# TensorE's order in a planned two-block network: float32 matmuls gathered, a turn of type charged, sums of one bank in order

## The chip, the core and the metric

The kernel runs on one core of a Trainium2 chip. The metric is the device time of one execution in microseconds (us). The kernel before was timed three times: 2192.33, 2192.88 and 2197.85 us, the median is 2192.88 us.

## What is computed

One sequence of 256 tokens of width 1024 passes through two residual blocks of two layers each, all in float32. Each layer is a feed-forward network of 2816, a mixer, and a second feed-forward network.

```python
def first_block(x, ...):                       # twice (DEPTH = 2)
    h = rmsnorm(x, ffn1_pre_g[l])
    x = x + 0.5 * rmsnorm(swiglu(h, ffn1_w_gate[l], ffn1_w_up[l], ffn1_w_down[l]), ffn1_post_g[l])
    h = rmsnorm(x, mix_pre_g[l])
    m = hybrid_mixer(h, w_in[l], w_out[l], ...)   # gated delta net, differential attention, SSD, mLSTM
    x = x + rmsnorm(m, mix_post_g[l])
    ...                                           # ffn2 as ffn1
def second_block(x, c, w_ada, b_ada, ...):     # twice
    mod = cond @ w_ada[l] + b_ada[l]              # nine rows of shifts, scales and gates
    y = _swiglu(_modulate(x, sh1, sc1), ffn1_w_gate[l], ffn1_w_up[l], ffn1_w_down[l])
    x = _post_norm(x, y, g1, FFN_RES, ln_gain[l, 0], ln_bias[l, 0])
    y = _token_mixer(_modulate(x, sh2, sc2), w_in[l], w_out[l])  # retention, dilated and stick-breaking attention
    ...
```

## The kernel before

Weights come from memory in units of 128 x 1024 (tiles `raw`, `R`, `S`), fetched by SyncE's queue. ScalarE rounds each unit to float32r (`wH`), VectorE takes the difference (`wL`), and activations are split likewise (`hT`, `A`, `B`, `X`: a high and a low part each). Every large product is then three float32r matmuls (`mm3`, `ws3`: high by high, high by low, low by high), summed in one PSUM bank. These are 12408 of the program's 13728 matmuls. The other 1320 read float32: 444 transposes with the identity (`tr<-con,h` and the like, 128 x 128) and 876 small products of the mixers. Of these small products 628 use a part of the array (64 rows by 64 columns in the gated delta net, 32 or 64 rows in the attentions), the others all 128 x 128 of it. A float32 product that is not a transpose has two records in the trace.

PSUM banks have names by use: `pa`, `pb` for the feed-forward sums, `pj` for the mixers' projections, `pg` and `po` for the small products and the last projection of a mixer, `tr` for transposes. The mixers' code is a set of generators (`gdn`, `diff`, `ssd`, `mlstm`; `retention`, `dilated`, `stick`) woven between the projections, so that float32r matmuls stand between the links of their chains of small products.

No instruction is issued while this code runs. `Program` records every operation as an `Op` with its engine, the time that it occupies it (`occ`), the time until its result (`done`; both from `taken`) and what it must follow. `emit` then plans: `ranks` gives each operation the longest way from it to the end, with TensorE's operations tied in their present order; `place` puts all operations on timelines of the engines by rank; TensorE's order is then sorted by the planned starts, and this is done four times (`ROUNDS`). The best plan's starts order the instructions of all engines, and each engine runs its own in that order. So a table of costs and the rules of `emit` set the order of every engine, DMA issues too. All recorded operations carry one source line, that of `getattr(...)` in `Engine.__getattr__`.

Before the change, the line that orders TensorE anew at the end of a round is

```python
pe = sorted(pe, key=lambda o: (o.start, o.i))
```

and a float32r matmul of m columns is charged `max(0.12, m / 2400 + 0.0127)` us: 0.12 at 256 columns, 0.226 at 512.

Of the kernel before, what the change touches and what calls it, by code (L numbers as in the profile page):

```python
# [13 lines left out]
F32R = mybir.dt.float32r  # L14
# [3 lines left out]
PSUM = bass.MemoryType.PSUM  # L18
# [166 lines left out]
class Tile:  # L185


    def __init__(self, pool, name, shape, dt, tag, bufs):
        self.pool, self.name, self.shape, self.dt, self.tag, self.bufs = pool, name, shape, dt, tag, bufs
        self.space = PSUM if pool is not None and tag in Program.banks else None  # L190
        self.size = math.prod(shape[1:]) + -math.prod(shape[1:]) % 8
        self.host, self.at = None, 0
        self.ap, self.seen, self.gates, self.gate, self.ops = None, [], None, None, []

    def real(self):
        if self.ap is None:
# [64 lines left out]


class Op:
    __slots__ = ("i", "eng", "run", "occ", "done", "before", "after", "start", "end", "rank", "size", "ins", "outs")

    def __init__(self, i, eng, run, occ, done, size=0):
        self.i, self.eng, self.run, self.occ, self.done, self.size = i, eng, run, occ, done, size
        self.ins, self.outs = (), ()
        self.before, self.after, self.start, self.end, self.rank = {}, [], 0.0, 0.0, 0.0


class Program:
# [147 lines left out]
    def touch(self, op, v, write):  # L420
        t = v.tile
        held = t
        if t.pool is None:
            r = 0, 1, v.offset, v.offset + sum(s * (n - 1) for s, n in v.ap) + 1
        else:
            r = Clock.region(v)
        if t.host is not None:
            held = t.host
            r = (r[0], r[1], r[2] + t.at, r[3] + t.at)
        if write and held.gates is not None:  # L430
            g = held.gates
            if g.gate is None:
                g.gate = self.add(None, None)
                for u in g.ops:
                    self.after(g.gate, u)
            self.after(op, g.gate, 0.0)
        keep = []
        for q, o, w in held.seen:
            hit = q[0] < r[1] and r[0] < q[1] and q[2] < r[3] and r[2] < q[3]
            if hit and o is not op and (write or w):  # L440
                same = o.eng == op.eng == "pe"
                self.after(op, o, o.occ if same else None)
            if not (write and hit and r[0] <= q[0] and q[1] <= r[1] and r[2] <= q[2] and q[3] <= r[3]):
                keep.append((q, o, w))
        keep.append((r, op, write))
        held.seen = keep
# [13 lines left out]
    def ranks(self, pe):  # L460
        for op in self.ops:
            op.after = []
        for op in self.ops:
            for o, lag in op.before.items():
                o.after.append((op, lag))
        nxt = {a: b for a, b in zip(pe, pe[1:])}
        self.sorted = self.topo(nxt)
        for op in reversed(self.sorted):
            r = op.done
            for o, lag in op.after:  # L470
                r = max(r, lag + self.flight(op) + o.rank)
            if op in nxt:
                r = max(r, op.occ + nxt[op].rank)
            op.rank = r

    @staticmethod
# [23 lines left out]
    def place(self):  # L500

        free = {e: Timeline() for e in ("pe", "act", "dve", "pool", "sp", "actq", "wire")}
        for op in sorted(self.sorted, key=lambda o: -o.rank):
            t = 0.0
            for o, lag in op.before.items():
                t = max(t, o.start + (o.end - o.start - o.done) + lag)
            if op.eng is None:
                op.start, op.end = t, t
                continue
            op.start = free[op.eng].take(t, op.occ)  # L510
            op.end = op.start + op.done
            if op.size:
                b = op.size / DMA_RATE
                at = free["wire"].take(op.start + DMA_FIRST, b)
                op.end = at + b + DMA_LAST
        return max(op.end for op in self.ops)

    def emit(self):
        self.rooms()
# [2 lines left out]
        self.says = []  # L522
        best = None
        for _ in range(ROUNDS):
            self.ranks(pe)
            end = self.place()
            self.says.append(round(end, 1))
            if best is None or end < best[0]:
                best = (end, {op: op.start for op in self.ops})
            pe = sorted(pe, key=lambda o: (o.start, o.i))  # L530
        start = best[1]
        with self.tc.manual_schedule(), \
                self.tc.tile_pool(name="psum", bufs=1, space=PSUM, reuse_waits="tile") as self.psum.live, \
# [32 lines left out]
def taken(kind, name, outs, ins, a, k):  # L566

    n = max(math.prod(x.shape[1:]) for x in outs + ins)
    if kind == "pe":
# [1 line left out]
        if name == "transpose":  # L571
            return 0.11, 0.31
        if ins[1].dtype == F32R:
            occ = max(0.12, m / 2400 + 0.0127)
            return occ, occ + 0.2
        rows = ins[0].shape[0]
        occ = 2 * max(0.112, m / 1200 + 0.01)
# [35 lines left out]
}  # L613

LAG = 0.06
ROUNDS = 4
DMA_RATE = 0.3e6
DMA_FIRST, DMA_LAST = 0.3, 1.7
# [2 lines left out]
class Engine:  # L621
# [5 lines left out]
    def __getattr__(self, name):  # L627
        def call(*a, after=0.0, **k):
# [16 lines left out]
                op = self.prog.add(eng, run, 0.06, 0.06, size)  # L645
            else:
                op = self.prog.add(self.kind, run, *taken(self.kind, name, outs, ins, a, k))
            op.ins, op.outs = ([v for v in x if isinstance(v, View)] for x in (ins, outs))
            return op
        return call  # L650
# [1672 lines left out]
```

## Time and profile before

| what | us |
|---|---|
| median of three runs (lowest, highest) | 2192.88 (2192.33, 2197.85) |
| the profiled execution's own time | 2192.09 |
| its span, first to last instruction | 2190.3 |
| busy in the span: TensorE matmuls, VectorE, ScalarE, GpSimd | 2142.4, 1614.9, 1021.6, 48.4 |
| two feed-forward networks between two mixers, one of three such stages | 388.2 |
| mixer of the first block, one of two | 184.7 |
| mixer of the second block, one of two | 127.2 |

The granted TensorE clock has a mean of 0.998 of full speed. Matmuls overlap in the records (each lasts longer than the distance to the next one), so this text counts distances from start to start. Idle times in brackets in a timeline are those of the engine, and behind the arrow stands what ended them.

### The profile page before, as it was taken

The numbers are of one execution on the slowest core, as the hardware profiler recorded it, in microseconds if no ns is written. First come the engines' busy times: TensorE is split into PE (matmuls) and PEld (weight loads), VectorE is DVE, ScalarE is ACT, GpSimd is POOL, SyncE is SP. The second block draws the span as 40 slices with busy tenths as digits, with TensorE's granted clock in tenths as the row PEclk, the third lists the DMA queues.
The fourth block names the chain that finished last, engine by engine and source line by source line (L and its number), as shares of the span: only waits on it lengthen the run. The fifth ranks groups of instructions, "written<-read, shape, count | busy, mean of one in ns | idle before, by whom it ended". The sixth has DMA issues, their size and how long they took to land. (4 is left out here: it accounts for less than half of the span.)

```text
span 2190.3 us, 36375 instructions
## 1 busy us (share of the span) xinstructions
PE 2142.4 (98%) x14604; PEld 1909.5 (87%) x14604; DVE 1614.9 (74%) x2301; ACT 1021.6 (47%) x1440; POOL 48.4 (2%) x73
## 2 busy tenths in 40 slices
PE   8999999999999999999999999999999999998998
PEld 7997988898799888879988988878988998876996
DVE  6676897777776779877768667778678766869654
ACT  6444634544454445454444443644443443544441
POOL 0000001000000000010000000000000000000000
PEclk9999999999999999999999999999999999999999
DMA  9785524778686851467787775548676776547661
GB/s 341 248 290 164 147 59 145 249 231 273 219 266 207 281 156 55 130 199 238 249 270 254 220 265 157 173 155 281 220 255 231 251 231 194 165 148 229 213 195 63
DMA packets 208313, 455.30 MB, mean 208 GB/s; under 512 B 20808, under 2 KB 56008, under 8 KB 208144
## 3 DMA queue, kind: packets, MB, share of 16 engines
q1 hardware_dynamic: 207856, 451.87, 63.5%
q8 instruction: 114, 1.87, 0.4%
q10 hardware_dynamic: 288, 1.11, 0.1%
q14 instruction: 55, 0.45, 0.1%
HBM read 451.80 MB, written 1.12 MB: 207 GB/s over the span
## 5 line engine op out<-in xcount | busy, mean ns | idle before, releaser
L639 PE MATMUL pa<-hT,wH 128*128 128x256 f32 x3008 | 546.3, 283 | 0.0
L639 DVE TENSOR_TENSOR wL<-raw,wH 128x1024 fp32r<-128x1024 f32 (+1 forms) x362 | 422.9, 1179 | 160.9 <-ACT wH L639 158.8
L639 ACT CAST wH<-raw 128x1024 fp32r<-128x1024 f32 (+1 forms) x362 | 363.9, 1015 | 375.3 <-PE pa L639 133.9
L639 PEld LDWEIGHTS pa<-hT,wH 128*128 128x128 f32 x3008 | 468.9, 192 | 2.5 <-issue 0.9
L639 PE MATMUL pa<-hT,wL 128*128 128x256 f32 x1504 | 425.1, 283 | 0.0
L639 PE MATMUL pa<-hT,X 128*128 128x256 f32 x2400 | 306.3, 282 | 0.0
L639 PEld LDWEIGHTS pa<-hT,X 128*128 128x128 f32 x2400 | 296.2, 188 | 2.0 <-issue 1.2
L639 PEld LDWEIGHTS pa<-hT,wL 128*128 128x128 f32 x1504 | 288.5, 192 | 0.0
L639 PE MATMUL pj<-wH,hT 128*128 128x256 f32 (+1 forms) x768 | 202.0, 340 | 2.1 <-DVE G L639 1.2
L639 DVE TENSOR_TENSOR X<-raw,X 128x1024 fp32r<-128x1024 f32 (+1 forms) x106 | 121.6, 1147 | 60.9 <-ACT X L639 60.6
L639 DVE TENSOR_TENSOR wL<-R,wH 128x1024 fp32r<-128x1024 f32 (+1 forms) x111 | 129.9, 1174 | 40.7 <-ACT wH L639 39.3
L639 PEld LDWEIGHTS pj<-wH,hT 128*128 128x128 f32 x768 | 132.3, 189 | 24.5 <-issue 5.8
L639 ACT CAST wH<-R 128x1024 fp32r<-128x1024 f32 (+1 forms) x111 | 111.5, 1008 | 86.4 <-PE pa L639 44.1
L639 ACT CAST X<-raw 128x1024 fp32r<-128x1024 f32 (+1 forms) x106 | 104.6, 987 | 98.0 <-PE pa L639 64.0
L639 PE MATMUL pa<-wH,hT 128*128 128x512 f32 x384 | 131.1, 402 | 1.1 <-ACT hT L639 1.0
L639 PE MATMUL pj<-hT,wH 128*128 128x256 f32 (+1 forms) x672 | 126.8, 288 | 0.1
L639 PE MATMUL pj<-wL,hT 128*128 128x256 f32 (+1 forms) x384 | 125.8, 328 | 0.0
L639 DVE SCALAR_TENSOR_TENSOR aacc<-raw,cols,aacc 128x1024 f32<-128x1024 f32 x78 | 99.8, 1279 | 12.4 <-DMA raw<-in_w_ada_dram 12.0
L639 PEld LDWEIGHTS pj<-hT,wH 128*128 128x128 f32 (+1 forms) x672 | 102.3, 186 | 3.3 <-issue 0.7
L639 PE MATMUL pb<-wH,A 128*128 128x512 f32 x288 | 102.2, 395 | 0.0
L639 PE MATMUL pa<-wH,A 128*128 128x512 f32 x288 | 102.2, 395 | 0.0
L639 PE MATMUL pj<-hT,wL 128*128 128x256 f32 (+1 forms) x336 | 95.0, 283 | 0.0
(420 smaller groups left out, 3426.6 us busy)
## 6 DMA issues: line engine op xcount, KB each, us to landing
raw<-in_ffn_w_gate_dram SPq DMA_DIRECT2D x114, 512.0 KB
raw<-in_w_in_dram SPq DMA_DIRECT2D x108, 512.0 KB
raw<-in_ffn_w_down_dram SPq DMA_DIRECT2D x107, 512.0 KB
raw<-in_w_ada_dram SPq DMA_DIRECT2D x88, 512.0 KB
raw<-in_ffn_w_up_dram SPq DMA_DIRECT2D x84, 512.0 KB
R<-in_ffn_w_up_dram SPq DMA_DIRECT2D x56, 512.0 KB
R<-in_ffn_w_down_dram SPq DMA_DIRECT2D x52, 512.0 KB
R<-in_w_ada_dram SPq DMA_DIRECT2D x40, 512.0 KB
```

Of the source, the lines that this page charges most:

```text
L639: getattr(self.prog.tc.nc, self.eng).__getattribute__(name)(*[real(x) for x in a], **{q: real(x) for q, x in k.items()})
```

## The change

Five things are edited. (1) `taken` charges a float32r matmul 0.12 us up to 256 columns and 0.232 us above. (2) An operation of TensorE is marked `plain` when its second operand is not float32r, transposes included, and `turn` = 0.05 us is added to the time of each one whose neighbour before it is of the other kind. (3) An operation that is one of several matmuls of one sum is marked `many`, and each operation that writes a PSUM tile follows the one recorded before it on that tile if either is `many`. (4) After each round's sort, `gather` goes through TensorE's order: behind a plain operation it pulls forward other plain ones that are planned within 4 us (`SPAN`) and whose inputs the plan has ready. (5) In a second pass it holds plain operations back, until just before the next plain one, where the plan has nobody waiting for them sooner. The computation is the same.

```diff
+        if write and t.space == PSUM and op.eng == "pe":
+            if t.sums and (op.many or t.sums[-1].many):
+                self.after(op, t.sums[-1], t.sums[-1].occ)
+            t.sums.append(op)
...
-                r = max(r, op.occ + nxt[op].rank)
+                r = max(r, op.occ + op.turn + nxt[op].rank)
...
-            op.start = free[op.eng].take(t, op.occ)
-            op.end = op.start + op.done
+            op.start = free[op.eng].take(t, op.occ + op.turn)
+            op.end = op.start + op.turn + op.done
...
+    def gather(self, pe):
+        out, todo = [], dict.fromkeys(pe)
+        while todo:
+            op = next(iter(todo))
+            del todo[op]
+            out.append(op)
+            if not op.plain:
+                continue
+            t = op.end - op.done + op.occ
+            for o in list(itertools.islice(todo, 64)):
+                if o.start > t + SPAN:
+                    break
+                if o.plain and all(b not in todo and b.start + (b.end - b.start - b.done) + lag <= t
+                                   for b, lag in o.before.items()):
+                    del todo[o]
+                    out.append(o)
...
+            for a, b in zip([pe[0]] + pe, pe):
+                b.turn = TURN * (a.plain != b.plain)
...
-            pe = sorted(pe, key=lambda o: (o.start, o.i))
+            pe = self.gather(sorted(pe, key=lambda o: (o.start, o.i)))
...
-            occ = max(0.12, m / 2400 + 0.0127)
+            occ = 0.12 if m <= 256 else 0.232
...
+TURN = 0.05
+SPAN = 4.0
...
+                op.many = name == "matmul" and not (k["start"] and k["stop"])
+                op.plain = self.kind == "pe" and ins[1].dtype != F32R
```

The source line of all operations moves from 639 to 696. Counted over both programs, TensorE's 12408 float32r matmuls stand in the same order among themselves but for four that move by at most 22 places. Runs of plain operations between float32r matmuls go from 176 to 138. SyncE's 976 DMAs and the instructions of VectorE and ScalarE are the same ones, some of them in another order.

TensorE, end of a feed-forward network (the first one), where the tail's `h` is transposed for the next stage between the last float32r matmuls of the second token half. Before:

```order
L639 MATMUL pa<-X,B 128x512 x12
L639 MATMUL pa<-A,B 128x512 x7
L639 MATMUL tr<-con_71,h 128x128 x4
L639 MATMUL pa<-A,B 128x512
L639 MATMUL tr<-con_71,h 128x128 x4
L639 MATMUL pa<-A,B 128x512 x10
```

After:

```order
L696 MATMUL pa<-X,B 128x512 x12
L696 MATMUL pa<-A,B 128x512 x6
L696 MATMUL tr<-con_71,h 128x128 x8
L696 MATMUL pa<-A,B 128x512 x12
```

The four transposes of each half of `h` now follow each other, and the float32r matmul ahead of them and the one between them stand behind them. The same is found at the end of five more of the eight feed-forward networks.

TensorE, mixer of the first block, a piece of the gated delta net (`pg`, 64x64) with the other heads' small products (`po`) between projections (`pj`). Before:

```order
L639 MATMUL pg<-L,B 64x64 x2
L639 MATMUL pj<-hT_259,wH 128x256
L639 MATMUL po<-G,con_71 128x4
L639 MATMUL pg<-L,B 64x64 x2
L639 MATMUL po<-con_71,G 128x128 x4
L639 MATMUL pg<-L,B 64x64 x12
L639 MATMUL po<-S 128x256 x2
L639 MATMUL pg<-A,B 64x64 x8
L639 MATMUL pj<-hT_266,wH 128x256
```

After:

```order
L696 MATMUL po<-G,con_71 128x4
L696 MATMUL pg<-L,B 64x64 x8
L696 MATMUL po<-con_71,G 128x128 x4
L696 MATMUL po<-S 128x256
L696 MATMUL pg<-A,B 64x64 x8
L696 MATMUL pj<-hT_266,wH 128x256
L696 MATMUL pj<-hT_259,wL 128x256
L696 MATMUL pj<-hT_259,wH 128x256
L696 MATMUL pj<-hT_266,wH 128x256
L696 MATMUL po<-S 128x256
L696 MATMUL pg<-A,B 64x64 x8
```

Eight of the `pg<-L,B` were pulled into an earlier run, the two `po<-S` (32 rows of the array) stand apart now, and each is followed by eight of 64x64.

End of the second mixer of the second block, where the last projection (`pg<-wH,X` and on) takes the transposed heads' outputs; TensorE and SyncE. Before:

```order
L639 MATMUL pg<-wH,X 128x512
L639 MATMUL pg<-wL,X 128x512
L639 MATMUL tr<-con_71,A 128x128 x2
L639 MATMUL tr<-con_71,R 128x128 x2
...
L639 DMA S<-mods 128x1024
L639 DMA raw<-in_w_out_dram 128x1024
L639 DMA arow<-in_b_ada_dram 1x512
```

After:

```order
L696 MATMUL pg<-wH,X 128x512
L696 MATMUL tr<-con_71,A 128x128 x2
L696 MATMUL tr<-con_71,R 128x128 x2
L696 MATMUL pg<-wL,X 128x512
...
L696 DMA S<-mods 128x1024
L696 DMA arow<-in_b_ada_dram 1x512
L696 DMA raw<-in_w_out_dram 128x1024
```

On TensorE one float32r matmul moved behind four transposes; on SyncE the last unit of `w_out` moved behind a small DMA.

## Rows read from the trace of the kernel before

**Rows 1.** The page: busy time, share of the span, instructions.

```profile
PE 2142.4 (98%) x14604; PEld 1909.5 (87%) x14604; DVE 1614.9 (74%) x2301; ACT 1021.6 (47%) x1440; POOL 48.4 (2%) x73
```

**Rows 2.** Stages: window, length, busy time of each engine, clock, DMA share, GB/s.

```profile
204.20:388.90 184.70, 178.75 (x1607) 158.21 (x1605) 153.85 (x371) 92.15 (x183) 11.49 (x17) 1.00 0.40 118
388.90:777.10 388.20, 386.12 (x2519) 348.75 (x2519) 281.99 (x311) 185.80 (x239) 5.27 (x8) 1.00 0.75 246
```

**Rows 3.** TensorE's waits in the first mixer: total us, times, longest.

```profile
PE pg L639 <- DVE B L639: 1.8, 5, 0.4
PE pg L639 <- DVE A L639: 1.2, 4, 0.5
```

**Rows 4.** TensorE's timeline, transposes among float32r matmuls: start, busy, count.

```profile
619.89 0.60 PE L639 MATMUL tr<-con,G 128*128 128x128 f32 x4
620.25 0.49 PE L639 MATMUL pa<-hT,wH 128*128 128x256 f32 x2
620.57 0.29 PE L639 MATMUL pa<-hT,wL 128*128 128x256 f32 x1
...
620.93 0.28 PE L639 MATMUL pa<-hT,wL 128*128 128x256 f32 x1
```

**Rows 5.** TensorE's groups: shapes, count, busy us, mean ns of one, idle before.

```profile
L639 PE MATMUL tr<-con,G 128*128 128x128 f32 x192 | 29.3, 276 | 5.0 <-DVE G L639 4.7
```

**Rows 6.** TensorE's timeline, eight float32 products of the whole array.

```profile
1398.89 0.40 PE L639 MATMUL pj<-wH,hT 128*128 128x512 f32 x1
...
1400.41 0.39 PE L639 MATMUL po<-R,B 128*128 128x64 f32 x2
1400.63 0.39 PE L639 MATMUL po<-A,B 128*128 128x64 f32 x2
...
1401.14 0.39 PE L639 MATMUL pj<-wL,hT 128*128 128x512 f32 x1
```

**Rows 7.** TensorE's timeline, sixteen products of 64 x 64.

```profile
314.33 0.28 PE L639 MATMUL pj<-wH,hT 128*128 128x256 f32 x1
314.54 1.15 PE L639 MATMUL pg<-A,B 64*64 64x64 f32 x32
...
315.84 0.28 PE L639 MATMUL pj<-wL,hT 128*128 128x256 f32 x1
```

**Rows 8.** TensorE's timeline, two shapes of part of the array in one run.

```profile
290.13 1.15 PE L639 MATMUL pg<-A,B 64*64 64x64 f32 x32
291.21 0.70 PE L639 MATMUL po<-S 32*128 32x256 f32 x4
292.21 0.68 PE L639 MATMUL pg<-A 64*64 64x64 f32 x16 [0.30 <-DVE A L639]
```

**Rows 9.** TensorE's timeline, a step of the gated delta net.

```profile
326.59 0.28 PE L639 MATMUL pg<-G,B 64*64 64x64 f32 x2
327.19 0.33 PE L639 MATMUL pg<-G,B 64*64 64x64 f32 x2 [0.32 <-DVE B L639]
```

**Rows 10.** Timeline, end of the second feed-forward network: start, busy, engine.

```profile
578.96 1.75 PE L639 MATMUL pa<-A,B 128*128 128x512 f32 x7
...
580.07 1.42 DVE L639 SCALAR_TENSOR_TENSOR h<-x,rr,L 128x512 f32<-128x512 f32 x2 [0.73 <-POOL rr L639]
...
580.87 0.66 PE L639 MATMUL tr<-con,h 128*128 128x128 f32 x4 [0.17 <-DVE h L639]
...
581.61 0.60 PE L639 MATMUL tr<-con,h 128*128 128x128 f32 x4
```

**Rows 11.** TensorE's timeline, end of the first mixer of the second block.

```profile
1452.27 0.44 PE L639 MATMUL tr<-con,A 128*128 128x128 f32 x2 [0.23 <-DVE X L639]
```

**Rows 12.** Timeline, end of the second mixer of the second block; SPq is SyncE's queue.

```profile
1966.79 0.37 SPq L639 DMA_DIRECT2D raw<-in_w_out_dram  x1
...
1967.21 0.28 SPq L639 DMA_DIRECT2D arow<-in_b_ada_dram  x1
...
1972.79 0.74 PE L639 MATMUL pg<-wH,X 128*128 128x512 f32 x2 [2.25 <-ACT wH L639]
```

More of the change, by code (lines that the diff above doesn't have):

```diff
@@ L192, in __init__ @@
         self.host, self.at = None, 0
-        self.ap, self.seen, self.gates, self.gate, self.ops = None, [], None, None, []
+        self.ap, self.seen, self.gates, self.gate, self.ops, self.sums = None, [], None, None, [], []
     def real(self):
@@ L263 @@
 class Op:
-    __slots__ = ("i", "eng", "run", "occ", "done", "before", "after", "start", "end", "rank", "size", "ins", "outs")
+    __slots__ = ("i", "eng", "run", "occ", "done", "before", "after", "start", "end", "rank", "size", "ins", "outs", "plain", "turn", "many")
     def __init__(self, i, eng, run, occ, done, size=0):
         self.i, self.eng, self.run, self.occ, self.done, self.size = i, eng, run, occ, done, size
-        self.ins, self.outs = (), ()
+        self.ins, self.outs, self.plain, self.turn, self.many = (), (), False, 0.0, False
         self.before, self.after, self.start, self.end, self.rank = {}, [], 0.0, 0.0, 0.0
@@ L516, in place @@
         return max(op.end for op in self.ops)
+    def gather(self, pe):
[14 more added lines that the diff above has]
+                    out.append(o)
+        late, nxt = {}, {}
+        for o in sorted((o for o in self.ops if o.eng != "pe"), key=lambda o: (-o.start, -o.i)):
+            t = min([(b.start if b.eng == "pe" else late.get(b, b.start)) - lag - (o.end - o.start - o.done)
+                     for b, lag in o.after] + [math.inf])
+            if o.eng is not None:
+                t = min(t, nxt.get(o.eng, math.inf) - o.occ)
+                nxt[o.eng] = max(t, o.start)
+            late[o] = max(t, o.start)
+        pe, out, held = out, [], []
+        for i, op in enumerate(pe):
+            if op.plain:
+                out += held
+                held = []
+                t = min([(b.start if b.eng == "pe" else late[b]) - lag for b, lag in op.after] + [math.inf])
+                j = next((j for j in range(i + 1, len(pe)) if pe[j].start > t or pe[j].plain), len(pe))
+                op_late = j < len(pe) and pe[j].plain and j > i + 1 and pe[j].start <= t
+                out.append(op)
+                if op_late:
+                    run = [out.pop()]
+                    while out and out[-1].plain and min([(b.start if b.eng == "pe" else late[b]) - lag for b, lag in
+                                                         out[-1].after] + [math.inf]) >= pe[j].start:
+                        run.insert(0, out.pop())
+                    if out and out[-1].plain:
+                        out += run
+                    else:
+                        held = run
+            else:
+                out.append(op)
+        return out + held
     def emit(self):
```

## The prediction

> **What bounds the kernel now.** I read the page first: matmuls are in flight on TensorE for 98% of the span, VectorE is busy for 74% [rows 1]. The reader is to see that only TensorE's own time and its waits can matter, and that a full row says nothing of waits, since records overlap. Next come the stages [rows 2]. Between two mixers TensorE is busy in 386 of 388 us; the order of the float32r matmuls is the same there after the change, so those stages can change at their seams alone. A mixer of the first block has 6 of its 185 us without a matmul in flight. Third, the waits inside that mixer [rows 3]: nine waits of the small products (`pg`) for VectorE, 3.0 us in all. Last, timelines, where the distance from a start to the next start gives the price of a turn between the two types. The change names such a price, 0.05 us, and orders TensorE by it; so the first question is whether the trace has it.
>
> **What a turn costs.** Four transposes among float32r matmuls [rows 4]: from their start to the `wL` matmul at 620.57 are 0.68 us, in which two more float32r matmuls lie. Three float32r matmuls take 0.36 us (620.57 to 620.93), 0.12 each, so the four transposes took 0.68 - 0.24 = 0.44, or 0.11 each. The row's own busy time, 0.60, less the length of the last, 0.276 on the mean of its group [rows 5], leaves 0.32 for three steps: also 0.11. Both turns together cost nothing. Eight float32 products of the whole array [rows 6]: 1398.89 to 1401.14 is 2.25 us with two float32r matmuls of 512 columns in it. These take 0.23 each ([rows 10]: seven in 1.75, less the last one's 0.39, is 1.36 / 6). That leaves 1.79, or 0.224 for each; the distance of two pairs of records inside the run is 0.22. Nothing again.
>
> Sixteen products of 64 x 64 [rows 7] differ: 314.33 to 315.84 is 1.51 us, less two float32r matmuls 1.27. Such a row of sixteen is busy for 1.15, one of eight for 0.68 [rows 8], so eight take 0.47 and sixteen 0.94. That leaves 0.33 us for the two ends, 0.17 each. The cost hangs on the shape, not on the type: a change between the whole array and a part of it costs about 0.17 us, and a turn between float32r and float32 on the whole array about 0.
>
> [...]
>
> **The change, part by part.**
>
> *Turns.* Counted over both orders, turns of type fall from 351 to 275, but changes between whole and part of the array only from 172 to 168, and changes between two shapes of part of the array rise from 12 to 24 (32-row and 64-row products among 64 x 64, as in the second place shown of the order). The first: 4 x 0.17 = 0.7 us saved. For the second: from the sixteen at 290.13 to the 32-row pair at 291.21 are 1.08 us, against 0.94 for sixteen [rows 8], so entering costs 0.14, and leaving can't be told from the wait there. Bounds are 0.1 and 0.33 (as much as both ends of a run in the whole array); I take 0.2, nearer the entry. 12 x 0.2 = +2.4. **Sum +1.7**, from +0.5 to +3.4.
>
> *Waits inside the delta net.* Five waits end on VectorE's `B` and four on `A` in each mixer of the first block [rows 3]. The five are a product that comes right behind another in the same bank, with a VectorE read of that bank put between them: 0.60 us from start to start [rows 9] against 0.1 without, so 0.5 each. In the changed order I count four such places instead of five. Of the four for `A`, three come in the same distance behind their producers as before; the one at 292.21 (0.30 idle) goes [rows 8], since another run of eight now stands before it. That is 0.5 and, with a restart of about 0.2 as between 0.32 idle and 0.5 lost [rows 9], another 0.5: 1.0 us a mixer; two mixers: **-2.0**. Bounds: 0 (new waits replace them) and -6.0 (all 3.0 us go, twice).
>
> *Seams of the feed-forward networks.* In six of them two float32r matmuls that stood ahead of and between the transposes now stand behind them. VectorE makes the halves of `h` in 1.42 us from 580.07, so one at 580.78 and one at 581.49 [rows 10]. The transposes wait for them (0.17 idle at 580.87), and the second four start at 581.61, right behind the second half. Both moved matmuls filled time in which TensorE would have waited: without them the first four still start at 580.87, the second at about 581.58, and two matmuls of 0.23 us are left over: +0.45. Three seams look like this one; at the other three the first transposes follow with no idle time, and the move costs 0 to 0.45. I take 3 x 0.45 = **+1.35**, bounds 0 (a later half of `h` costs nothing if the stage behind waits anyway) and +2.7.
>
> *End of the mixers of the second block.* The transposes at 1452.27 wait 0.23 us for VectorE's `X` [rows 11], behind a float32r matmul that now comes after them: 0.23 more idle, in two mixers **+0.46** (0 to 0.46).
>
> *SyncE.* At the end of the last mixer TensorE waits 2.25 us for the rounding of a unit of `w_out` whose DMA was issued at 1966.79 [rows 12]. Now a small DMA, issued at 1967.21 before, is ahead of it in the queue: one issue with its gap, **+0.4** on a wait that nothing covers. Bounds 0 (if TensorE itself gets there later) and +0.4.
>
> *Costs of long passes.* 0.232 in place of 0.226 us moves planned times alone, and a wait of sums for each other in one bank adds no instruction and leaves the float32r order as it was. 0, hidden by nothing since nothing is issued for it; what they can do is in the counts above.
>
> All sums are made against the profiled execution's 2192.09 us: 0 + 1.7 - 2.0 + 1.35 + 0.46 + 0.4 = +1.9, so 2194.0. That execution is 0.8 below the median of the runs shown; carried to it, 2192.88 + 1.9 = **2194.8 us**.
>
> **The rivals.** A difference under 0.3%, 6.6 us, is about what a measurement of this kernel can't tell from none (its three runs lie 0.25% apart).
>
> *The turn of type itself costs.* Of the 76 turns that go, 24 are at transposes and 52 at products of part of the array. Had their 0.17 us been paid for the type and not for the shape, 52 of them would save 8.8 us, and with the other terms (+0.2 without the first) the time would be 2184.3. For it: 124 of the 172 changes between whole and part in the order before are also turns of type. Against it: the change from one float32 shape to another costs 0.14 with no turn of type in it [rows 8], and a turn without a change of shape costs nothing [rows 4 to 6]. With it goes the chance that nearly all the delta net's waits vanish, since other products now stand between its links: -6.0 in place of -2.0 gives 2190.8, still no change. 0.16 for a time of 2186 and below.
>
> *Gathered products wait at the head of the queue.* Pulling a product forward to the moment at which the plan has its inputs ready takes away the float32r matmuls that stood before it. If VectorE runs later than planned, by one weight unit in its queue, the product waits with everything behind it. The weights' differences are such units, and the 1.42 us for two halves of `h` [rows 10] is the nearest row that prices them from below: some 0.7 to 1.2 us a wait. I count four places in each mixer of the first block and two in each of the second where a product was brought nearer to its producer: 12 places. Slower than 0.3% needs 4.7 us beyond the sum, that is five to seven of them late; eight late ones at 0.9 give 2202. Against it: the old order put products at the planned moment too, and lost 3.0 us a mixer to it. 0.22.
>
> *The forecast*, between the two: 0.62.
>
> **How the numbers follow.** The best bounds added up, +0.5 - 6.0 = -5.5, give 2187.4; the worst, 3.4 + 2.7 + 0.46 + 0.4 = +7.0, give 2199.9. The range goes from 2186, where the first rival's cases of partial price begin, to 2203, which takes in the second rival's 2202; the first rival in full and more than eight late products are left out, some 2 in 10. The chances: faster by over 0.3% 0.16, within 0.3% 0.62, slower by over 0.3% 0.22.
>
> **What would show it.** In the profile after, runs of 64 x 64 products should still show 0.33 us for their two ends, and transposes none. The stages of feed-forward networks should be 388 us with 0 to 1 added; the mixers of the first block 184 to 186; the `pg` waits for `B` four in place of five. The prediction is wrong if a mixer of the first block changes by more than 2 us, or the second block's by more than 1, either way: by fewer waits than counted, or by a tail that waits for a VectorE chain that the gathering made later or earlier.

## The result, and the profile after

The changed kernel took 2209.24 us (median of four runs, 2206.32 to 2212.03), against 2192.9: a ratio of 1.0067, 95% interval 1.0055 to 1.0079. It is slower by 16 us, where the prediction had +1.9 and a range up to 2203. The mean granted clock of the runs was 0.991 to 0.994; the kernel before had 0.994 to 0.998. The profiled execution of the change took 2206.32 us with a span of 2204.5, 14.2 more than the span of before.

The page's first part answers to [rows 1]: busy time of each engine, share of the span, instructions.

```profile
PE 2151.8 (98%) x14604; PEld 1918.1 (87%) x14604; DVE 1615.5 (73%) x2301; ACT 1021.3 (46%) x1440; POOL 50.3 (2%) x73
```

The same 14604 records keep TensorE busy for 9.4 us longer. The other engines did the same work. So 9.4 of the 14.2 us lie in what the records take, the rest in time without a matmul in flight. The stages say where. A stage runs from its first matmul to the first of the next; columns as in [rows 2], the clock is the number before the DMA share.

```profile
204.60:393.60 189.00, 182.06 (x1608) 161.67 (x1606) 154.48 (x371) 92.41 (x185) 12.41 (x17) 0.98 0.39 115
393.60:782.70 389.10, 386.60 (x2519) 348.79 (x2520) 282.37 (x311) 186.00 (x238) 5.26 (x8) 1.00 0.75 245
782.70:970.50 187.80, 181.67 (x1608) 161.44 (x1606) 154.19 (x371) 92.60 (x185) 11.52 (x17) 0.98 0.39 119
```

The first mixer is 4.3 us longer than in [rows 2] and the feed-forward pair (FFN) 0.9. Both first-block mixers stand at a clock of 0.98 where before showed 1.00. Narrow windows of the same view show what a clock of 0.98 consists of:

```profile
343.10:349.90 6.80, 6.05 (x56) 5.34 (x55) 5.40 (x12) 1.85 (x4) 0.00 (x0) 1.00 0.68 218
349.90:356.70 6.80, 6.80 (x29) 5.90 (x30) 4.96 (x15) 0.90 (x3) 2.12 (x2) 0.50 0.21 45
356.70:363.50 6.80, 6.80 (x61) 6.67 (x61) 4.80 (x16) 2.79 (x4) 2.14 (x3) 1.00 0.38 125
926.80:933.60 6.80, 6.80 (x30) 5.90 (x30) 5.04 (x15) 0.90 (x3) 2.12 (x2) 0.50 0.14 57
1984.90:1988.30 3.40, 3.06 (x7) 2.48 (x8) 3.04 (x3) 0.29 (x1) 0.00 (x0) 0.50 0.88 289
2012.20:2019.00 6.80, 6.11 (x19) 4.35 (x18) 5.68 (x9) 1.26 (x3) 0.64 (x1) 0.50 0.74 231
```

In the window at 349.9 and the last three the granted clock is 0.50, half of full speed. These are the four half-speed stretches of the change, 23.9 us together (further on the text says that the clock fell there); the profiled execution of before has one, 3.4 us at 961.1, at 0.51. Both have one more behind their last matmul, at 0.50 (from 2183.1 in before and 2199.9 in the change). In 6.8 us at half the clock TensorE gets 29 records done; in the 6.8 us after it, 61 of another mix.

TensorE's waits in the first mixer (total us, times, longest) answer to [rows 3], and places of the timeline to [rows 8 to 12]:

```profile
PE pg L696 <- DVE A L696: 2.0, 3, 0.9
PE pg L696 <- DVE B L696: 1.5, 4, 0.4
PE pg L696 <- ACT B L696: 0.3, 1, 0.3
PE tr L696 <- DVE R L696: 0.3, 1, 0.3
```

```profile
300.10 0.68 PE L696 MATMUL pg<-A 64*64 64x64 f32 x16 [0.85 <-DVE A L696]
308.61 0.90 PE L696 MATMUL pg<-A 64*64 64x64 f32 x15 [0.90 <-DVE A L696]
...
585.51 1.32 PE L696 MATMUL tr<-con,h 128*128 128x128 f32 x8 [0.39 <-DVE h L696]
...
1161.90 0.33 PE L696 MATMUL tr<-con,h 128*128 128x128 f32 x1 [1.23 <-DVE h L696]
...
1463.04 0.44 PE L696 MATMUL tr<-con,A 128*128 128x128 f32 x2 [1.30 <-DVE X L696]
...
1978.97 0.29 SPq L696 DMA_DIRECT2D arow<-in_b_ada_dram  x1
1979.37 0.33 SPq L696 DMA_DIRECT2D raw<-in_w_out_dram  x1
...
1985.24 1.65 PE L696 MATMUL pg<-wH,X 128*128 128x512 f32 x3 [3.22 <-ACT wH L696]
```

The `B` waits are four in place of five, as counted, and 0.3 us less. But the `A` waits are 0.8 more, in fewer and longer pieces, and two small waits are new. At 585.51 all eight transposes of `h` stand in one run, with 0.39 us of wait ahead in place of 0.17. At 1463.04 the transposes wait 1.30 us for `X` in place of 0.23; the 512-column matmul that stood ahead of them is now behind. The small DMA does stand before `w_out`, and the wait there is 3.22 us in place of 2.25.

### The profile page after: what moved, and what is told of

Read it like the earlier page. It is cut to its first block, busy times and chain, and to the rows that moved or that the text cites. A ratio compares the mean times of both kernels' runs of the same rounds, so it can differ in the third digit from the quotient of the medians.

```text
span 2204.5 us, 36369 instructions
## 1 busy us (share of the span) xinstructions
PE 2151.8 (98%) x14604; PEld 1918.1 (87%) x14604; DVE 1615.5 (73%) x2301; ACT 1021.3 (46%) x1440; POOL 50.3 (2%) x73
## 3 DMA queue, kind: packets, MB, share of 16 engines
q8 instruction: 114, 1.87, 0.3%
```

## The experiments

Two theories went in. **The clock:** the new order lets TensorE's clock fall where it did not before. **The order alone:** the edits make waits and worse seams at full clock. Each run stands beside runs of before on the same chip, with a median between 2193.56 and 2194.37 us for the job. This table has the stage lengths (us) of the traces; a star marks a stage with a half-speed stretch in it. Each experiment has a label in brackets, by which the text names it.

| stage | before | change | times alone | turn, sums | old times | first mixer | mixer filled |
|---|---|---|---|---|---|---|---|
| first FFN | 195.8 | 196.5 | 196.7 | 196.1 | 196.6 | 196.7 | 197.4 |
| mixer, block 1 | 184.8 | 189.0* | 184.8 | 187.4* | 188.9* | 186.2 | 187.3 |
| FFN pair | 388.2 | 389.1 | 389.1 | 388.6* | 388.6 | 389.0* | 389.0* |
| mixer, block 1 | 184.1 | 187.8* | 184.3 | 185.4 | 188.0* | 185.3 | 186.0 |
| FFN pair | 387.8* | 388.7 | 391.3* | 387.8 | 387.8 | 389.1 | 390.9* |
| mixer, block 2 | 122.1 | 123.0 | 122.1 | 122.4 | 122.0 | 122.9 | 122.9 |
| FFN pair | 387.3 | 387.5 | 388.5* | 387.3 | 387.3 | 387.6 | 390.0* |
| mixer, block 2 | 127.2 | 128.9* | 128.7* | 128.1* | 128.3* | 129.3* | 128.9* |
| last FFN | 195.5 | 196.7* | 196.1* | 197.4* | 197.0* | 197.1* | 196.8* |

Behind the change the columns are the kernels e3, e13, e11, e6 and e12.

**Without the gathering (e1).** Turn, sums and new times stay.

```diff
-            pe = self.gather(sorted(pe, key=lambda o: (o.start, o.i)))
+            pe = sorted(pe, key=lambda o: (o.start, o.i))
```

> All of the change but the gathering: TensorE's order is the plain sort by planned starts again, the turn is still charged, sums stay in order and the longer passes have their truer time. Theory C (gathering makes stretches of small float32 work after which the granted clock falls to half for some microseconds, and that is most of the loss): about 2196 us, no stretch at half clock in the mixers of the first block but the one short one that the kernel before has; what is left over the kernel before is the 2.5 us that the seams of the feed-forward networks cost, since the eight transposes in a row stand in this order too. Theory W (the loss is in waits that come from gathered products behind VectorE): about 2196 us as well. Rival R (the rest of the change, its costs and the order of sums, makes the loss): about 2206 us.

Measured 2203.71 us, ratio 1.0042 (1.0027 to 1.0057). Gathering is not most of the loss: 10.1 us stay without it. The first-block mixers take 185.8 and 186.4 us, with one half-speed stretch of 3.4 us at 914.3.

A run with the gathering alone (e2: old times, no charge for a turn, no order of sums) gave no time. In its order a product starts a new sum in a PSUM bank in which another sum is still open, where edit (3) keeps the sums of a bank in order. So no run here prices the gathering by itself.

**The new times alone (e3).** Gathering, turn and sums out; 0.232 us for 512 columns stays.

```diff
-            if t.sums and (op.many or t.sums[-1].many):
+            if False and t.sums and (op.many or t.sums[-1].many):
...
-TURN = 0.05
+TURN = 0.0
...
-            pe = self.gather(sorted(pe, key=lambda o: (o.start, o.i)))
+            pe = sorted(pe, key=lambda o: (o.start, o.i))
```

> The truer time of long passes alone, without gathering, turn or order of sums. The order has the eight transposes in a row at all six seams, so it prices them: 2.5 us over the kernel before, about 2195.5 us, if the seams cost what the traces of before and after say (0.42 to 0.45 at three, 0.11 to 0.15 at three, 0.8 at one more). If about 2193, the seams cost nothing by themselves. Rival R: 2200 or more.

Measured 2199.96 us, 1.0027 (1.0018 to 1.0036): 6.4 us for an edit that adds no instruction. The mixers of the first block have the order of before, instruction for instruction, and stand within 0.2 us of it; the loss is in the FFN and, 1.5 us, in the last mixer. The second FFN pair, 391.3 us, holds a half-speed stretch behind a wait of a transpose for `h`. That wait is 0.45 us before, 1.23 in the change and 2.3 here.

**Gathered by shape (e4).** Only float32 products on a part of the array count as plain, all else is the change's.

```diff
-                op.plain = self.kind == "pe" and ins[1].dtype != F32R
+                part = self.kind == "pe" and (ins[0].shape[0] < P or math.prod(ins[0].shape[1:]) < P)
+                op.plain = part and ins[1].dtype != F32R
```

> Gathering and the charge of a turn go by the part of the array instead of the type: only float32 products that use part of it (64 or 32 rows or columns) are gathered, transposes and float32 products of the whole array count as float32r ones. Changes between whole and part fall to 144 (168 in the change, 172 before). My price of 0.17 us a change: 28 x 0.17 = 4.8 us less than before, 14 more changes between two parts cost 2.8, the seams 2.5: about 2193.5 us if no clock is lost and no wait comes anew. Theory C: longest run 4.3 us, so no half clock, 2191 to 2196. Theory W: gathered products wait here too, 2198 or more at full clock.

Measured 2196.27 us, 1.0009 (0.9998 to 1.002). Changes of shape fall to 144 (172 before, 168 in the change), the mixers take 186.0 and 185.2 us, and the FFN pairs keep 389.1 and 389.4. A half-speed stretch lies in each mixer, against theory C, although the longest run is shorter.

**The kernel before, profiled again (e5).** No edit.

> The kernel before, unchanged, profiled once more. Theory (the granted clock): the mean clock stands between 0.994 and 0.998, as in its timed runs, and where it is below 0.998 there is at least one half-speed stretch more than the one at 961.1, after a long TensorE wait at a layer's end or a stage's start; the two first-block mixers hold none and keep 184 to 185 us. Rival (the order of instructions alone makes the loss): every stage within 0.3 us of the first profile, and the clock the same.

Measured 2193.09 us, clock 0.997. The stretch at 961.1 is missing and two others are there:

```profile
1974.10:1977.50 3.40, 3.40 (x10) 2.59 (x9) 3.26 (x5) 0.00 (x0) 0.00 (x0) 0.51 0.84 280
2001.40:2004.80 3.40, 3.00 (x11) 2.47 (x12) 2.76 (x5) 1.17 (x2) 0.00 (x0) 0.51 0.70 251
```

Both lie behind waits for weights that the first profile shows too (2.25 us ahead of 1972.79, 1.86 us ahead of 1998.98). So with one order the clock fell at one place in one execution and at two others in the next. The stages that keep the full clock in both profiles agree to 0.1 us.

The pair at 961.2 takes 387.8 us in both, with the stretch and without. First a row of before, then two of this profile:

```profile
974.47 1.29 PE L639 MATMUL tr<-con,G 128*128 128x128 f32 x8 [0.33 <-DVE G L639]
```

```profile
972.60 0.50 PE L639 MATMUL pa<-wL,hT 128*128 128x512 f32 x1 [1.04 <-DVE wL L639]
974.43 1.29 PE L639 MATMUL tr<-con,G 128*128 128x128 f32 x8 [0.40 <-DVE G L639]
```

At full clock TensorE comes earlier to a product whose weights aren't ready, and waits 1.04 us there. With the stretch it comes later and doesn't wait, and by the transposes of `G` the two are level again.

The timed runs price the clock without a change of order. Of the 70 runs of before in these jobs, the 14 with a mean clock of 0.998 took 2191.9 to 2193.4 us, the 11 with 0.994 took 2197.0 to 2198.6: some 5 us for the same instructions.

**Gathering in the first mixer alone (e6).** Both passes of `gather` leave operations planned after 600 us as they are.

```diff
-            if not op.plain:
+            if not op.plain or op.start > 600:
...
-            if op.plain:
+            if op.plain and op.start < 600:
```

> The change with the gathering kept in the first mixer alone: that mixer's TensorE order is word for word that of the changed kernel, with its run of 27 float32 products; the second mixer goes back nearly to the order of before (1172 of 1232 instructions in place); the FFN keeps the seams of the change. Theory (the granted clock falls in the long float32 run): a half-speed stretch of 3.4 to 6.8 us near 350 us and none in the second mixer; first mixer 187 to 189 us, second 184 to 185.5; median about 2202, with 2199 to 2206. Rival 1 (gathered products wait at the head of the queue): the first mixer is 188 to 189 us with the clock at full speed. Rival 2 (the clock falls at random after waits): the stretch near 350 is missing, the first mixer is 185.5 at most, and the falls lie elsewhere.

Measured 2204.29 us, 1.0053 (1.0038 to 1.0069). The first mixer has the change's order, instruction for instruction, and this execution kept the full clock in it. First the timeline of the change at the place, then that of this kernel:

```profile
349.81 0.62 PE L696 MATMUL po<-B,S 128*128 128x65 f32 x2
350.22 0.63 PE L696 MATMUL po<-A 128*128 128x65 f32 x2
350.65 0.63 PE L696 MATMUL po<-B,S 128*128 128x65 f32 x2
351.21 0.69 PE L696 MATMUL pg<-B,A 128*64 128x128 f32 x2
...
354.35 0.58 PE L696 MATMUL pj<-wH,hT 128*128 128x256 f32 x1
```

```profile
350.36 0.43 PE L696 MATMUL po<-B,S 128*128 128x65 f32 x2
350.63 0.39 PE L696 MATMUL po<-A 128*128 128x65 f32 x2
350.85 0.39 PE L696 MATMUL po<-B,S 128*128 128x65 f32 x2
351.17 0.43 PE L696 MATMUL pg<-B,A 128*64 128x128 f32 x2
...
352.92 0.39 PE L696 MATMUL pj<-wH,hT 128*128 128x256 f32 x1
```

From the first of these rows to the float32r matmul are 4.54 us at half the clock and 2.56 at full clock: the same products, 1.8 times as long. The mixer takes 186.2 us here and 189.0 in the change, so this fall costs 2.8 us and the new order itself 1.4 over before (184.8). Of those, 1.3 are waits: the groups of TensorE's waits in the mixer sum to 7.1 us, in before to 5.8. None of the three came out whole: the stretch was not there (rival 2), but the mixer is not down to 185.5; and waits at the head of the queue do cost something at full clock (rival 1), about half of what the fall costs in the change.

**Short runs of float32 (e7).** After 2.5 us of float32 the gathering places six float32r instructions; the longest run is planned at 3.7 us in place of 6.0.

```diff
+            if op.plain and took > 2.5:
+                fill = [o for o in itertools.islice(todo, 96) if not o.plain and o.start < op.start + SPAN
+                        and all(b not in todo for b in o.before)][:6]
+                for o in fill:
+                    del todo[o]
+                    out.append(o)
+                took = 0.0
...
+                    if took > 2.5:
+                        break
+                    took += o.occ
```

> The change with float32 runs cut short: after 2.5 us of float32 in a row the gathering places six float32r instructions. The longest run is then 3.7 us in place of 6.0, and the number of turns is 311 (275 in the change, 351 before). All else is the changed kernel's. Theory (the granted clock): no half-speed stretch in either first-block mixer, each of them 184.5 to 186 us, where the changed kernel takes 189.0 and 187.8; FFN pairs still 389; median about 2201, with 2197 to 2205. Rival 1 (head-of-queue waits of gathered products): the mixers keep 187 us or more with the clock at full speed, median above 2205. Rival 2 (fewer turns were worth something): slower than the change, above 2209.

Measured 2206.11 us, 1.0057 (1.0043 to 1.0071). The clock fell at 339.0 and 352.6 in the first mixer and at 929.5 in the second, 3.4 us each, and the mixers took 189.5 and 187.4 us. My theory that the length of an unbroken float32 run decides is refuted. With 311 turns in place of 275 the kernel is not slower than the change, where 0.17 us for each of the 36 would have been 6.1 us. A price of the 0.05 us in the code, 1.8 us, can't be told from this run: its half-speed stretches in these mixers are 3.4 us shorter, and the mixers together as long (376.9 against 376.8).

**By shape, old times (e8).** As e4, with 0.226 us again.

> Gathered by shape (only float32 on a part of the array counts as plain), with the old 0.226 us for a pass of 512 columns. The FFN's order is then that of before, instruction for instruction; the shape changes stay at 144 against 172. Theory (the seams of the new times cost 0.4 us each and each layer-end wait is a chance for the clock to fall): FFN pairs back to 388.2, 387.8 and 387.3, the median 3 us under that of the by-shape kernel with the new times, about 2193, with 2189.5 to 2195. Rival (the new times cost nothing, the clock alone moved): 2196, as with them, FFN pairs at 389.

Measured 2193.47 us, 1.0001 (0.9992 to 1.001). The FFN pairs are back at 388.6, 387.8 and 387.3, and 2.8 us are gained on e4. The second block's mixers take 121.2 and 126.2, less than before; five half-speed stretches take that gain back, the last of them in a last FFN of 197.6 us.

**The change once more (e9).** No edit.

> The changed kernel, unchanged, profiled and timed once more, to see which of its half-speed stretches belong to its order and which to one execution. Theory (the order sets where the clock can fall, the execution whether it does): the stretch at the last layer's start (near 2012 us) and at the end of the last mixer (near 1985) are there again, those at 349.9 and 926.8 are there or not; where one is missing, that mixer is 186 to 186.5 us. Rival (the long float32 run makes it fall each time): both at 350 and 927 again, 189 and 188 us. Median 2206 to 2211 in both, mean clock 0.991 to 0.994.

Measured 2208.0 us, 1.0056 (1.0042 to 1.007), clock 0.991 to 0.994. Seven half-speed stretches, among them those of 349.9, 926.8, 1984.9 and 2012.2 again (2 to 6 us later here), and one at 1164.7 behind a wait of 2.47 us for `h`. Both first-block mixers fell again, as the rival had it; but e6 has the first one's order and didn't fall, so the order doesn't decide alone. The row of 1164.7:

```profile
1164.96 1.33 PE L696 MATMUL tr<-con,h 128*128 128x128 f32 x5 [2.47 <-DVE h L696]
```

**Two waits filled (e10).** Before two products that wait for weights, the product ahead of each is issued again, 12 and 7 times. They are added into two sums, so the kernel prices the waits and leaves the right values out.

```diff
                 if op.run is not None:
                     op.run()
+                    if op.eng == "pe":
+                        for _ in range({12432: 12, 12526: 7}.get(nth, 0)):
+                            op.run()
+                        nth += 1
```

> The changed kernel with TensorE kept busy in two waits: before the product that waits 3.2 us for w_out at the last mixer's end the product ahead of it is issued 12 times more, and before the one that waits 1.9 us for the last FFN layer's weights 7 times more (231 ns each, 2.8 and 1.6 us, inside the waits). They add to sums of the result, so two sums hold other values. Theory (the idle wait is what lets the clock fall there): no half-speed stretch at 1985 and 2012; the last mixer 127.3 to 128 us in place of 128.9, the last FFN 195.3 to 196 in place of 196.7; median 1.5 to 3 us under the changed kernel's in the same job. Rival (the clock falls there whatever TensorE does, or its loss is hidden by the waits anyway): both stretches stay or the median stays within 1 us of the changed kernel's.

Measured 2205.49 us, 1.0047 (1.0035 to 1.006), against 2208.0 for the change in the same job; the runs overlap. The place in the last FFN shows it best: first the change, then this kernel, timeline and then the window of the stage.

```profile
2011.51 0.50 PE L696 MATMUL pa<-wL,hT 128*128 128x512 f32 x1 [1.87 <-DVE wL L696]
...
2012.82 0.63 PE L696 MATMUL pa<-wH,hT 128*128 128x512 f32 x1
```

```profile
2009.62 2.21 PE L701 MATMUL pa<-wH,hT 128*128 128x512 f32 x9
2012.12 0.50 PE L701 MATMUL pa<-wL,hT 128*128 128x512 f32 x1 [0.28 <-DVE wL L701]
...
2013.15 0.39 PE L701 MATMUL pa<-wH,hT 128*128 128x512 f32 x1
```

```profile
1998.70:2194.10 195.40, 193.01 (x1254) 174.08 (x1252) 122.87 (x139) 77.88 (x91) 1.85 (x2) 1.00 0.57 183
```

The same wait stands in the kernel before at 1998.98, 1.86 us. Filled, the clock stays at 1.00 there, and the stage takes 195.4 us in place of 196.7. At the mixer's end the stretch is gone too, but the stage gains 0.4 us only (128.5), less than expected.

**The change with the old times (e11).** Gathering, turn and sums stay.

```diff
-            occ = 0.12 if m <= 256 else 0.232
+            occ = max(0.12, m / 2400 + 0.0127)
```

> The change without its new times of long passes (0.226 us again for 512 columns); gathering, turns and sums stay. The eight-transpose runs at the FFN's seams stay 24 in number, as in the change, and the run of 27 float32 products too. Theory (the seams come with any of the edits that moves the plan, and cost 0.4 us each at the first five): FFN pairs 389 and 388.7, median as the change within 2 us, 2205 to 2211. Rival (the new times alone are what the FFN pays for): FFN pairs back to 388.2 and 387.8, median 2203 to 2205.

Measured 2203.64 us, 1.0041 (1.0027 to 1.0056). My theory fell and the rival holds but for 0.4 us in one pair: FFN pairs 388.6, 387.8 and 387.3, and 4.4 us less than the change in the same job. It is the new times that the FFN pays for. The mixers fell at 350.7 and 927.6 and take 188.9 and 188.0, as in the change.

**The long float32 run filled (e12).** Four float32r products of 256 columns ahead of four products of the run, in both first-block mixers.

```diff
+            pes = [op for op in order if op.eng == "pe" and op.run is not None]
+            fill = {pes[n + d]: pes[2296 + d] for d in (0, 3750) for n in (2279, 2284, 2286, 2290)}
...
+                    for _ in range(4 if op in fill else 0):
+                        fill[op].run(start=True, stop=True)
                     op.run()
```

> The changed kernel with four float32r products of 256 columns (120 ns each) issued at four places inside the run of 27 float32 products, in both first-block mixers: ahead of the products at 347.8, 348.7, 349.6 and 351.2 us of the first mixer, two of which wait 0.38 and 0.37 us at the head of the queue. They write a bank that the next sum overwrites; nothing else moves. Their own price is 16 times 0.12, 1.9 us, less the 0.75 us of wait, some 1.2 us a mixer. Theory (a stretch with little but small float32 products lets the clock fall): no half-speed stretch near 350 and 927, the mixers 187 to 187.6 us for the first and 186.2 to 187 for the second (changed kernel: 189.0 and 187.8), median 1 to 4 us under the changed kernel's 2208. Rival (these falls have nothing to do with what TensorE does there): the stretches stay, the mixers are 190 and 189 us and the median 2 us over the changed kernel's.

Both mixers keep the full clock, and take what was expected, 187.3 and 186.0 us:

```profile
205.50:392.80 187.30, 181.12 (x1624) 160.94 (x1622) 154.54 (x371) 92.28 (x186) 12.41 (x17) 1.00 0.39 116
781.80:967.80 186.00, 180.86 (x1623) 160.84 (x1621) 154.15 (x371) 92.64 (x185) 11.52 (x17) 1.00 0.39 120
```

The price of the fill is 1.1 us (187.3 less 186.2 in e6). The median, 2208.26 us, 1.0057 (1.0041 to 1.0072), missed the expectation: it is that of the change. In the profile the clock fell elsewhere, at 1161.0 and 1495.5 in FFN pairs that take 390.9 and 390.0 us (388.7 and 387.5 in the change), and the first FFN is 0.9 us longer (197.4 against 196.5). So the gain shows in the two mixers and not in the time.

**Turn and sums alone (e13).** The old times and no gathering (the edits of e1 and e11 together).

> The turn's 0.05 us and the order of sums alone: no gathering and the old time of long passes. Theory (the FFN pays for the new times alone, the first-block mixers for the gathering): FFN pairs 388.2, 387.8 and 387.3; first-block mixers 184.5 to 186; median 2194 to 2200, the second-block mixers with up to 1.3 us more of the wait of a transpose for X. Rival (the two edits cost nothing): 2192 to 2194.

Measured 2199.45 us, 1.002 (1.0011 to 1.0029). The median and two of the FFN pairs are as the theory had them; the first mixer, 187.4 us in place of 186 at most, is not. Two edits that I had put at nothing cost 5.2 us, falls of the clock included. The transposes' waits for `X` in the second block are 0.5 and 0.4 us, that for `w_out` 3.1. The first mixer has a half-speed stretch of 3.4 us at 340.2, with no gathering at all.

**By shape, the two waits filled (e14)**, with transposes and products that were issued before, and **the kernel before, filled (e15)** in the same way.

```diff
+FILL = ((12434, 12408, 20), (12527, 12484, 7))
...
+            fill = {pes[n]: (pes[m], k) for n, m, k in FILL}
...
+                    for _ in range(fill[op][1] if op in fill else 0):
+                        fill[op][0].run(start=True, stop=True) if fill[op][0].many else fill[op][0].run()
                     op.run()
```

> Gathered by shape, old times, and the two waits of the last block filled with work that leaves the result as it is: 20 transposes (110 ns) issued again before the product that waits for w_out at the last mixer's end, 7 float32r products of 512 columns before the one that waits for the last FFN layer's weights. Theory (the clock falls where TensorE idles): no half-speed stretch near 1973 and 2000, last FFN 195.5 in place of 197.6, median 1.5 to 3 us under the 2193.5 of the same kernel without it, 2190 to 2192. Rival (transposes don't hold the clock, or the falls move on to the next wait): 2193 to 2194.

> The kernel before with the same two waits filled in the same way. Theory: no half-speed stretch near 1974 and 2001, mean clock of all runs 0.996 to 0.998, median 0.5 to 1.5 us under that of before, since before falls there in some executions only. Rival: same as before or slower, since the added products delay what waits.

Measured 2193.09 us, 0.9991 (0.9983 to 1.0), and 2194.16 us, 0.9996 (0.9987 to 1.0005). The median of before in this job is 2194.24, so filling it gained nothing. Neither place fell in either kernel; the last FFN is at 195.5 (197.6 in e8) and 195.8. But unfilled, these places fell in e5 and e8 and not in before and e4, so two filled profiles don't show that the fill did it. By shape, a new stretch of 6.8 us at 1484.4 made the FFN pair there 389.5 us, so the rival, that the falls move on, holds for half. No version here is shown to beat before: the best lies 0.1% under it, with an interval that reaches to no change.

## Why the prediction was wrong

*By edits*, medians against before in the same job: times alone +6.4 (e3), turn and sums +5.2 (e13), all three +10.1 (e1), gathering with turn and sums +9.3 (e11), everything +13.6 (e9) and +16.3 (the result). Gathering is then worth 3.5 (13.6 - 10.1) to 6.2 us (16.3 - 10.1).

*By causes*, in the profiled execution: a fall near 350 costs 2.8 us (189.0 against 186.2), one near 927 2.9 (187.8 against e12's 186.0 less its fill, taken at 1.1 as in the first mixer), the last FFN's 1.3 and the last mixer's 0.4 (both against e10). That is **7.4 us of the 14.2 for the clock**. The stretch of before at 961.1 costs nothing that the stage shows: 387.8 us with it, 387.8 without (e5). The other **6.8 us stand at full clock**, where the prediction had +1.9. The runs give a rough second split: at a mean clock of 0.994 the change took 2206.3 and 2208.0 us and before some 2198, which leaves about 9 us at equal clock. The profiled execution is also the fastest of the four, so the clock's share of the median's 16.3 us isn't settled by it.

*No term for the granted clock.* This is the step that put the time outside the range: 2209.24 less 7.4 is 2201.8, inside it, while 2209.24 less the 4.9 that the order was missed by (6.8 - 1.9) is 2204.3, still outside. "All sums are made against the profiled execution's 2192.09 us" carried durations read at a clock of 0.998 to an order that got 0.991 to 0.994. With 6.8 in place of 1.9 the forecast would have been 2199.7, inside the range. In the first-block mixers of the change's order the clock fell in 8 of 9 cases (profiles of the change, e6, e9, e10, e11), in before's in 1 of 8 (before, e3, e5, e15), and with float32r work put into the run in none of 2 (e12). So what TensorE does there matters, as far as so few cases show it; that the length of an unbroken float32 run decides is refuted by e7, and that it takes gathering is refuted by e13's fall at 340.2.

Ahead of the stretch at 2012.2 stands a wait of 1.87 us for weights, and the clock stayed at 1.00 there when it was filled (e10). Gaps of 0.38 and 0.37 us stand among small products ahead of 349.9, but e6 has gaps of 0.38 and 0.36 at the same place and kept the full clock. So with one order the clock fell in one execution and not in another, in the first mixer of the change and of e6, and at the places named in before and e5; no run here shows the reason.

*Costs of long passes: 0.* Wrong: +6.4 alone (e3). In the change the FFN pairs pay 0.9, 0.9 and 0.2 us at full clock, of which the old times give 0.5, 0.9 and 0.2 back (e11). The rest of the 6.4 lies in the first FFN and in e3's starred stages, by up to 3.5 us, where the clock fell; in two of these four it fell behind waits longer than before's (2.3 us against 0.45, 3.0 against 2.3).

*Sums in one bank and the turn's charge: 0.* Wrong: +5.2 (e13), of which the second first-block mixer shows 1.3 at full clock (185.4 against 184.1). That no instruction is added says nothing of what stands ahead of what.

*Waits inside the delta net, -2.0.* The sign is wrong: +1.3 us in the first mixer. Four `B` waits were counted rightly, and the wait at 292.21 [rows 8] is gone as read. But waits of 0.85 and 0.90 us at the head of the queue came: the second rival's mechanism, with its price of 0.7 to 1.2, at far fewer places than the eight that its 2202 needed. The prediction's own sign of being wrong, a first-block mixer changed by more than 2 us, came (+4.2), though not by either of the two causes that it names: most of it is the clock.

*Seams, +1.35.* (The seams are the ends of the feed-forward networks, where `h` is transposed.) Mechanism right, size too small: the seven seams' intervals grew by 2.5 us, 0.42 to 0.45 at the three that I had priced so, 0.77 at the one ahead of 1161.90, 0.1 to 0.15 at three. The upper bound, 2.7, holds.

*Transposes behind `X`, +0.46.* Measured +1.1 and +0.5: the matmul moved behind takes 0.23 us, but VectorE's `X` came later as well.

*SyncE, +0.4.* The order is as read, and the issue put ahead takes 0.40 us (1978.97 to 1979.37); but the wait grew by 0.97 (3.22 against 2.25), and where the rest comes from stays open.

*Turns, +1.7.* That a turn of type costs nothing rests on [rows 4] and [rows 6] as before; 36 more in e7 cost far less than 0.17 us each, and no run prices the turn closer. (The upper bound of this term is 12 x 0.33 - 0.7 = 3.3, not 3.4, which moves nothing.) The sixteen-product runs that should still show 0.33 us no longer stand alone among float32r matmuls, so that row was not seen again.

Open stays which property of the order lets the clock fall in a mixer, why the wait at 1165 is 1.23 us in one execution and 2.47 in another, and how much of the loss by edits is clock in each.

## What to carry to other kernels

Durations from one profile hold at the clock of that profile (before took some 5 us more at a mean clock of 0.994 than at 0.998). Before an order of TensorE is changed, look at its granted clock in narrow windows, find the places where it fell in any execution, and give the change a term or a range for new ones; then profile the same program twice. An edit to a planner's costs adds no instruction and can still be the dearest part: run each edit alone.

## What was not expected of the hardware

A half-speed stretch cost here what no wait in it or behind it took back, not its length: 2.8 us for 6.8 in a mixer full of products, 1.3 for 6.8 where part of it covers waits, nothing for the 3.4 at 961.1, in place of which e5 has a later wait of 1.04 us. In e10 the repeated products in a wait took no time of their own, and the clock stayed at 1.00 there (195.4 us against 196.7). In the profiles without falls at the filled places others stood elsewhere, at 1495.5 in e12 and 1484.4 in e14, and the medians gained less than the filled stages.
